# Moving a head's output gates between the two halves of its q, k, v projection

## The chip, the cores and the metric

The kernel runs on one core of a Trainium2 chip. The metric is the device time of one execution in microseconds (us), as the median of several runs; a profile is one further execution, read from its hardware trace.

## The reference, cut to what matters

One layer is computed (`DEPTH = 1`): gated differential attention over 1024 tokens, model width 1024, 16 heads with two 64-wide query/key halves and 128-wide values.

```python
h = rms_norm(x, norm_g)
q, k, v, z = jnp.split(h @ w_in, 4, axis=-1)          # 16 heads x 128 columns each
q = rms_norm(q.reshape(b, s, 16, 2, 64), q_norm_g) * 64 ** -0.5
k = rms_norm(k.reshape(b, s, 16, 2, 64), k_norm_g)
...
for blk in range(s // 128):                            # causal, ALiBi bias
    scores = einsum('bqhmd,bkhmd->bhmqk', qb, kb)
    probs = softmax(scores + bias)
    weights = probs[:, :, 0] - lam * probs[:, :, 1]
    outs.append(einsum('bhqk,bkhe->bqhe', weights, vb))
o = rms_norm(concatenate(outs), head_norm_g) * (1.0 - lam_0)
o = o.reshape(b, s, 2048) * silu(z)
return x + o @ w_out
```

The gate of a head is `silu(z)` for its 128 columns.

## The kernel before, in words

**Precision by splitting.** Each float32 operand of the projection is scaled and split in two float16 parts, high and low; a product is three matmuls (high by high, high by low, low by high). The normed input is kept transposed on chip, `hh` and `hl`, in two halves of 512 tokens (`c` = 0 and 1).

**The loop.** The main loop at the end of the function runs over the heads, odd ones first, then even ones. In turn `i` it interleaves, with `merge`, two generators: `attend` of the head before and `project` of this head. Each `yield` carries a weight, and `merge` advances whichever lags by the rates given (14.5 to 44.0). Heads 10, 12 and 14 (`LATE`) have their gates computed after the last projection, in `late_gates`; for the other 13 heads `project` computes them itself.

**project.** For each half `c`, four token blocks `t`: 24 matmuls (L404 to L406) into a PSUM tile `pg` of 384 columns (q, k, v together), then ScalarE copies q and k to `rw` (L456) and the high part of v to `vh` (L457), and VectorE makes the low part (L458). After four blocks `norm(c)` does the q, k RMSNorm: a square on ScalarE (L415), a reduction (L417), small steps (L95 to L103), a multiply (L422), the float16 split (L425, L426) and a transposing DMA into `qk` (L427) with two copies (L430). Then come the gates: `gate(..., c)` for `c` = 0 and 1, each 24 matmuls into a PSUM tile `pz` (L481 to L483) and a chain of six steps, ScalarE and VectorE in turn (L486 to L491), which reads `pz` up to its last step and leaves the gate in an SBUF tile `sz`. `pg` and `pz` share one ring of three PSUM buffers (`PSG = 3`).

**The next head's weights.** `project` also prepares the weights of the next head. `load_raw` issues eight DMAs on SyncE's queue (L136) into `raww`, of which there is one buffer. `split_w` is a generator that `prepare` advances by one step at a time: one square per block of columns on ScalarE (L160, which writes into the new `wsp` tile), a tiny matmul for the maximum (L169) into spare columns of the `pg` tile of the moment, small steps on VectorE (L172 to L185), then per block a high part on ScalarE (L206) and a low part on VectorE (q, k: L212) or GpSimd (v and gate: L209, L210). There are two `wsp` buffers. `prepare` is called after each `pg` block, and at every second step of the gates; the step with the tiny matmul can only go on where a `pg` tile is handed in, so not at the gates' calls.

**attend.** For each of eight query blocks: score matmuls (L603) into a ring of four PSUM tiles `pss`, VectorE adds the bias and takes the running minimum (L592), ScalarE the exponential (L609), VectorE and ScalarE make the weights (L612 to L619), and a DMA transposes them (L621). `values(0)` (L633 to L635) comes after block 5 and `head_norm(0)` after block 6; `values(1)` and `head_norm(1)` of a head are a tail that the next turn runs after its blocks 1 and 2. `values` ends in a copy and two squares (L639 to L644), `head_norm` in a logarithm, an exponential (L655, L656) and a multiply (L663), after which `finalize` multiplies by the gate on GpSimd (L571) and writes it to DRAM (L572).

**Who orders the engines.** The instructions of an engine are put in order before the run by a planner that simulates the engines: it takes what is ready by its own estimate, with the order of the code as priority. Code order is therefore a wish; data, buffers and the few pinned instructions are the bounds.

Of the kernel before, what the change touches and what calls it, by code (L numbers as in the profile page):

```python
# [9 lines left out]
F32 = mybir.dt.float32  # L10
# [7 lines left out]
P = 128  # L18
# [9 lines left out]
LATE = (10, 12, 14)  # L28
# [11 lines left out]
def diff_attention_kernel(  # L40
# [65 lines left out]
    heads = [h for h in range(NH) if h % 2 == 1] + [h for h in range(NH) if h % 2 == 0]  # L106
    place = {h: i for i, h in enumerate(heads)}

    with ExitStack() as main:
# [113 lines left out]
        with ExitStack() as pro:  # L223
# [65 lines left out]
            for t in range(NB):  # L289
                ht = hts[t]  # L290
                c, o = t // 4, (t % 4) * P
# [87 lines left out]
        def project(hd, wt, st):  # L379
# [52 lines left out]
            nx, prep = st["next"], []  # L432
# [12 lines left out]
                        return  # L445
                    prep.pop(0)

            for c in range(2):
                rw = tmp.tile([P, 2, 4, P], F32, name="rw", tag="rw", bufs=2)
                for t in range(4):  # L450
                    pb = ps_g.tile([P, 512], F32, name="pg", tag="pg")
                    pg = pb[:, :384]
                    for hf in range(2):
                        gemm_piece(pg, c, t * P, range(hf * 4, hf * 4 + 4))
                        if hf:
                            A.activation(rw[:, :, t], pg[:, :256].rearrange("p (s b) -> p s b", s=2), AF.Copy)  # L456
                            A.activation(vh[:, c * 4 + t], pg[:, 256:], AF.Copy, scale=vsc)  # L457
                            V.scalar_tensor_tensor(out=vl[:, c * 4 + t], in0=pg[:, 256:], scalar=vsc,  # L458
                                                   in1=vh[:, c * 4 + t], op0=ALU.mult, op1=ALU.subtract)
                            prepare(lambda: pb[:, 384:])  # L460
                        elif hd == heads[0]:
                            prepare(None)
                        yield 2.1
                norm(c, rw)
            if hd in LATE:
                while prep:
                    prepare(None)
                return
            for c in range(2):
                for k in gate(st, wt, 3, c):  # L470
                    if k % 2:
                        prepare(None)
                    yield 0.69
            while prep:
                prepare(None)

        def gate(st, wt, n, c):

            pz = ps_g.tile([P, 512], F32, name="pz", tag="pg")
            for k in range(KT):  # L480
                T.matmul(pz, wt["hi"][:, k, n], hh[c][:, k], start=k == 0, stop=False)  # L481
                T.matmul(pz, wt["hi"][:, k, n], hl[c][:, k], start=False, stop=False)  # L482
                T.matmul(pz, wt["lo"][:, k, n], hh[c][:, k], start=False, stop=k == KT - 1)  # L483
                yield k
            e = vp.tile([P, 512], F32, name="sz", tag="sz", bufs=3)
            A.activation(e, pz, AF.Exp, scale=wt["inv"][:, 1, n:n + 1])  # L486
            V.tensor_scalar(e, e, 1e18, None, ALU.min)
            A.activation(e, e, AF.Ln, bias=1.0)
            V.scalar_tensor_tensor(out=e, in0=pz, scalar=wt["inv"][:, 1, n:n + 1], in1=e, op0=ALU.mult, op1=ALU.max)
            A.activation(e, e, AF.Exp, scale=-1.0)  # L490
            V.scalar_tensor_tensor(out=e, in0=pz, scalar=wt["inv"][:, 0, n:n + 1], in1=e,  # L491
                                   op0=ALU.mult, op1=ALU.mult)
            st["z"].append(e)
# [80 lines left out]
        def attend(hd, st):  # L574
# [48 lines left out]
            def values(c, t):  # L623

                vh, vl = st["vh"], st["vl"]
                po = ps_o.tile([P, 512], F32, name="po", tag="po")
                row = 8 * (c + 1) * P
                for j in range(4 * c + 4):
                    il = max(0, j - 4 * c)
                    out = po[:, il * P:].rearrange("p (t q) -> p t q", q=P)  # L630
                    rh = view(t[:, il, j * P:], [[row, 4 - il], [1, P]])
                    rl = view(t[:, il, (4 * c + il + 1 + j) * P:], [[row + P, 4 - il], [1, P]])
                    T.matmul(out, vh[:, j], rh, start=j == 0, stop=False)  # L633
                    T.matmul(out, vl[:, j], rh, start=False, stop=False)
                    T.matmul(out, vh[:, j], rl, start=False, stop=j == 4 * c + 3)  # L635
                    if j % 2:
                        yield 6 * (4 - il) * P / 2400
                os = tmp.tile([P, 512], F32, name="os", tag="os")
                A.activation(os, po, AF.Copy, scale=st["unit"])  # L639
                sq = tmp.tile([P, 512], F32, name="sqo", tag="sqo")  # L640
                A.activation(sq, os, AF.Square)
                sqh = tmp.tile([P, 512], F32R, name="sqh", tag="sqh")
                e = V if hd == heads[-1] else G
                A.activation(sqh, os, AF.Square)  # L644
                sql = tmp.tile([P, 512], F32R, name="sql", tag="sql")
                e.tensor_tensor(sql, sq, sqh.bitcast(F32), ALU.subtract)  # L646
                pos["n"] = (os, sq, sqh, sql)
# [138 lines left out]
```

## Time and profile before

| | us |
|---|---|
| median of 3 runs (lowest, highest) | 1172.26 (1170.85, 1175.99) |
| the profiled execution, device time | 1178.97 |
| its span, first to last instruction | 1177.2 |
| TensorE (PE) busy in the span | 1114.4 (95%) |
| VectorE (DVE), ScalarE (ACT), GpSimd (POOL) busy | 910.7, 750.6, 268.8 |

The first 84 us hold the prologue and the first head's projection, which has no attention beside it. From 84 to 782 us twelve turns follow with gates and attention, some 58 us each; from 782 to 925 us the three turns of the late heads; then the late gates and the output projection. Matmuls overlap in the pipeline, so busy time is read together with the waits.

### The profile page before, as it was taken

To read this page: it belongs to the slowest core of one execution; us is meant where nothing else is said; L and a number is where in the kernel's file an instruction comes from. 1 tells how busy PE (TensorE), PEld (TensorE's weight loads), DVE (VectorE), ACT (ScalarE), POOL (GpSimd) and SP (SyncE) were. 2 spreads that over 40 slices of the span, in tenths; PEclk is the share of its full clock that TensorE was granted. 3 is DMA by queue.
4 is the path that set the end of the run, shared out by engine and by line. 5 is a ranking of instruction groups with operands and counts; after the bars stand their busy time and mean duration, and the time that the engine had idled before them with its cause. 6 is when DMAs were issued, how large, how long until landed. Compare 5 with 4: busy or idle time off the path is not lost.

```text
span 1177.2 us, 18460 instructions
## 1 busy us (share of the span) xinstructions
PE 1114.4 (95%) x6154; PEld 670.4 (57%) x6154; DVE 910.7 (77%) x2335; ACT 750.6 (64%) x1583; POOL 268.8 (23%) x210
## 2 busy tenths in 40 slices
PE   5799999999899999999999999999998987999998
PEld 3555554555455555454545555555555534788887
DVE  6877979798879798989798989797888897654111
ACT  3757678686868786868686868686768765230000
POOL 3121313131413131314131313212120302022000
PEclk7999999999999999999999999999999988999999
DMA  7343546454626364636463635263663456767342
GB/s 221 109 103 70 129 94 144 77 130 94 141 66 155 79 147 80 150 81 141 84 147 78 152 78 144 68 150 76 127 135 84 110 117 143 204 219 239 108 134 70
DMA packets 327887, 143.50 MB, mean 122 GB/s; under 512 B 225136, under 2 KB 307312, under 8 KB 327792
## 3 DMA queue, kind: packets, MB, share of 16 engines
q1 hardware_dynamic: 323040, 133.93, 47.8%
q10 hardware_dynamic: 4752, 8.39, 2.7%
q8 instruction: 48, 0.79, 0.3%
q14 instruction: 47, 0.39, 0.1%
HBM read 63.11 MB, written 16.25 MB: 67 GB/s over the span
## 4 chain that ended last, share of the span: by engine, by line
PE 49%; DVE 19%; ACT 11%; issue 7%; DMA 6%; POOL 3%; SPq 3%; ACTq 0%; DVEq 0%; POOLq 0%
PE pg L404 8%; PE pg L406 7%; PE pg L405 7%; PE pf L532 5%; PE pf L533 5%; PE pf L534 5%; DVE p L592 5%; DMA raww<-in_l_w_in_dram 3%; ACT wsp L206 3%; SPq L136 3%; PE pss L603 3%; ACT wsp L160 2%; DVE p L615 2%; ACT p L609 2%; POOL wsp L210 2%
## 5 line engine op out<-in xcount | busy, mean ns | idle before, releaser
L404 PE MATMUL pg<-wsp,h 128*128 128x384 f16 x1016 | 334.3, 329 | 9.0 <-DVE sz L491 7.3
L406 PE MATMUL pg<-wsp,h 128*128 128x384 f16 x1016 | 334.3, 329 | 2.7 <-DVE h L298 2.7
L405 PE MATMUL pg<-wsp,h 128*128 128x384 f16 x1016 | 334.1, 329 | 0.0
L609 ACT ACTIVATE p<-p,mn 128x128 f32<-128x128 f32 (+7 forms) x256 | 196.1, 767 | 39.1 <-DVE mn L592 39.0
L603 PE MATMUL pss<-qk 128*128 128x512 f16 (+3 forms) x768 | 166.5, 328 | 22.3 <-DVE mn L592 22.2
L592 DVE CUSTOM_DVE_ANT_0 p<-pss,toep,nsl 128x512 f32<-128x512 f32 (+3 forms) x256 | 160.9, 642 | 16.9 <-DMA wt<-p 8.6
L66 ACT ACTIVATE p<-p,rc 128x128 f16<-128x128 f32 (+7 forms) x128 | 98.5, 771 | 77.4 <-DVE p L615 73.6
L405 PEld LDWEIGHTS <-h 128*128 128x128 f16 x1016 | 100.0, 98 | 77.1 <-issue 17.5
L406 PEld LDWEIGHTS <-h 128*128 128x128 f16 x1016 | 100.1, 99 | 68.9 <-issue 3.0
L404 PEld LDWEIGHTS <-h 128*128 128x128 f16 x1016 | 100.0, 98 | 65.8 <-issue 4.1
L603 PEld LDWEIGHTS <-qk 128*128 128x128 f16 x768 | 70.8, 98 | 81.9 <-issue 30.3
L619 DVE SCALAR_TENSOR_TENSOR p<-p,rc,p 128x128 f16<-128x128 f32 (+7 forms) x128 | 108.5, 849 | 10.6 <-ACT p L66 9.2
L615 DVE SCALAR_TENSOR_TENSOR p<-p,rc,p 128x128 f32<-128x128 f32 (+7 forms) x128 | 108.5, 852 | 0.0
L646 POOL TENSOR_TENSOR sql<-sqo,sqh 128x512 fp32r<-128x512 f32 x30 | 41.0, 1366 | 265.0 <-ACT sqh L644 265.0
L481 PE MATMUL pz<-h,wsp 128*128 128x512 f16 x256 | 97.8, 382 | 1.5 <-DVE sz L491 1.5
L483 PE MATMUL pz<-h,wsp 128*128 128x512 f16 x256 | 97.8, 382 | 0.0
L482 PE MATMUL pz<-h,wsp 128*128 128x512 f16 x256 | 97.8, 382 | 0.0
L209 POOL TENSOR_SCALAR raww<-raww,scw 128x1024 f32<-128x1024 f32 x29 | 40.5, 1406 | 166.8 <-ACT wsp L206 142.1
L160 ACT ACTIVATE wsp<-raww 128x1024 f16<-128x1024 f32 x61 | 63.6, 1044 | 20.6 <-DMA raww<-in_l_w_in_dram 19.4
L571 POOL TENSOR_TENSOR sz<-sqo,sz 128x512 f32<-128x512 f32 x26 | 33.7, 1295 | 185.4 <-DVE sqo L663 156.2
L592 DVE CUSTOM_DVE_ANT_0 p<-pss,toep,mn 128x128 f32<-128x128 f32 (+3 forms) x128 | 75.1, 601 | 0.3 <-PE pss L603 0.3
L458 DVE SCALAR_TENSOR_TENSOR vl<-pg,vh 128x128 f16<-128x128 f32 x128 | 36.3, 284 | 45.7 <-ACT vh L457 45.5
(163 smaller groups left out, 2098.6 us busy)
## 6 DMA issues: line engine op xcount, KB each, us to landing
raww<-in_l_w_in_dram SPq DMA_DIRECT2D x96, 256.0 KB, 4.2
rawo<-in_l_w_out_dram SPq DMA_DIRECT2D x32, 256.0 KB, 4.7
qk<-qk SPq DMA_DIRECT2D x64, 128.0 KB, 2.3
raww<-in_l_w_in_dram SPq DMA_DIRECT2D x40, 192.0 KB, 3.8
g_dram<-sz SPq DMA_DIRECT2D x30, 256.0 KB, 2.3
rawg<-g_dram ACTq DMA_DIRECT2D x24, 256.0 KB, 4.1
xt<-in_x_dram SPq DMA_DIRECT2D x8, 512.0 KB, 4.5
xr<-in_x_dram SPq DMA_DIRECT2D x16, 256.0 KB, 3.4
```

What stands on the lines that cost most here:

```text
L66: A.activation(out, in_, AF.Copy, scale=scale)
L404: T.matmul(pg, a_h, w_h, start=k == 0, stop=False)
L405: T.matmul(pg, a_h, w_l, start=False, stop=False)
L406: T.matmul(pg, a_l, w_h, start=False, stop=k == KT - 1)
L481: T.matmul(pz, wt["hi"][:, k, n], hh[c][:, k], start=k == 0, stop=False)
L482: T.matmul(pz, wt["hi"][:, k, n], hl[c][:, k], start=False, stop=False)
L483: T.matmul(pz, wt["lo"][:, k, n], hh[c][:, k], start=False, stop=k == KT - 1)
L592: V.tensor_tensor_reduce(out=pm[m][:, o:o + w], in0=pss[:, :w], in1=toep[:, u:u + w], scale=nslope, scalar=3e38 if prev[m] is None else pr ...
L603: T.matmul(pss[m][:, :w].rearrange("p (t q) -> p t q", q=P), qk[:, c, 0, i % 4, m], qk[:, b, v, :w // P, m], start=v == 1, stop=v == 2)
L609: A.activation(pm[m][:, :n], pm[m][:, :n], AF.Exp, scale=-1.0, bias=prev[m], accum_out=sx[:, m:m + 1])
L615: V.scalar_tensor_tensor(out=p0, in0=p1, scalar=rc[:, 1:2], in1=p0, op0=ALU.mult, op1=ALU.add)
L619: V.scalar_tensor_tensor(out=pl[:, n:], in0=p0, scalar=rc[:, 0:1], in1=pl[:, :n], op0=ALU.mult, op1=ALU.subtract)
```

## The change

`project` runs `qkv(0)`, then both gates (not for late heads), then `qkv(1)`. `prepare` is called twice per block in `qkv(0)` of every head and once per block in `qkv(1)`. `sz` gets a fourth buffer, and the 512-wide tile `sqo` of `values` is taken from the ring of `norm`'s tile (`sqk`, two buffers).

```diff
-            for c in range(2):
+            def qkv(c):
                 rw = tmp.tile([P, 2, 4, P], F32, name="rw", tag="rw", bufs=2)
                 for t in range(4):
...
                             prepare(lambda: pb[:, 384:])
-                        elif hd == heads[0]:
+                        elif c == 0:
                             prepare(None)
                         yield 2.1
                 norm(c, rw)
-            if hd in LATE:
-                while prep:
-                    prepare(None)
-                return
-            for c in range(2):
-                for k in gate(st, wt, 3, c):
-                    if k % 2:
-                        prepare(None)
-                    yield 0.69
+            yield from qkv(0)
+            if hd not in LATE:
+                for c in range(2):
+                    for k in gate(st, wt, 3, c):
+                        if k % 2:
+                            prepare(None)
+                        yield 0.69
+            yield from qkv(1)
             while prep:
                 prepare(None)
...
-            e = vp.tile([P, 512], F32, name="sz", tag="sz", bufs=3)
+            e = vp.tile([P, 512], F32, name="sz", tag="sz", bufs=4)
...
-                sq = tmp.tile([P, 512], F32, name="sqo", tag="sqo")
+                sq = tmp.tile([P, 1024], F32, name="sqo", tag="sqk", bufs=2)[:, :512]
```

## Rows read from the trace of the kernel before

**Rows 1.** The page's busy time of each engine, share and instructions.
```profile
PE 1114.4 (95%) x6154; PEld 670.4 (57%) x6154; DVE 910.7 (77%) x2335; ACT 750.6 (64%) x1583; POOL 268.8 (23%) x210
```

**Rows 2.** Stretches: length, busy by engine (PE, PEld, DVE, ACT, POOL), PEclk, DMA, GB/s.
```profile
200.00:258.00 58.00, 56.08 (x320) 31.00 (x319) 47.22 (x125) 42.90 (x93) 15.05 (x10) 0.97 0.54 117
...
491.00:513.00 22.00, 20.22 (x121) 11.43 (x120) 19.77 (x57) 18.25 (x44) 1.27 (x1) 1.00 0.60 120
...
523.00:549.00 26.00, 26.00 (x144) 13.88 (x143) 25.05 (x66) 19.85 (x39) 12.13 (x8) 1.00 0.53 131
...
84.00:782.00 698.00, 677.35 (x3924) 377.96 (x3922) 595.83 (x1578) 528.24 (x1119) 179.21 (x119) 1.00 0.50 111
```

**Rows 3.** Waits of PE, 84 to 782: total us, times, longest us.
```profile
PE pss L603 <- DVE mn L592: 11.2, 11, 1.6
PE pg L404 <- DVE sz L491: 7.3, 8, 2.3
```

**Rows 4.** Waits of PE, 20 to 84.
```profile
PE pg L406 <- DVE h L298: 2.7, 1, 2.7
PE tp L295 <- DVE nlam L361: 2.6, 1, 2.6
```

**Rows 5.** Chain that ended last, around 441 and 499: start us, us, what.
```profile
440.80 0.32 PE pg L404
...
481.56 2.14 POOL wsp L210
...
488.40 5.42 DMA raww<-in_l_w_in_dram
...
494.56 3.23 ACT wsp L160 x6
497.79 0.53 ACT sz L490
...
499.15 0.32 PE pg L404
```

**Rows 6.** Groups by line, 84 to 782: count | busy us, mean ns | idle before.
```profile
L417 DVE TENSOR_REDUCE ssk<-sqk 128x16 f32<-128x1024 f32 x24 | 29.1, 1213 | 6.5 <-ACT sqk L415 6.5
L95 DVE TENSOR_SCALAR v_k<-ssk,ep 128x8 f32<-128x8 f32 x48 | 28.5, 637 | 0.4
L422 DVE TENSOR_TENSOR rw<-rw,r_k 128x1024 f32<-128x1024 f32 x24 | 30.1, 1255 | 1.2
L426 DVE TENSOR_TENSOR sqk<-rw,sqk 128x1024 f16<-128x1024 f32 x24 | 33.9, 1414 | 1.8 <-ACT sqk L425 1.8
L487 DVE TENSOR_SCALAR sz<-sz 128x512 f32<-128x512 f32 x24 | 10.8, 452 | 1.0 <-ACT sz L486 0.9
L489 DVE SCALAR_TENSOR_TENSOR sz<-pz,inv,sz 128x512 f32<-128x512 f32 x24 | 17.8, 743 | 0.4 <-ACT sz L488 0.4
L491 DVE SCALAR_TENSOR_TENSOR sz<-pz,inv,sz 128x512 f32<-128x512 f32 x24 | 17.9, 746 | 2.7 <-ACT sz L490 2.5
L212 DVE SCALAR_TENSOR_TENSOR wsp<-raww,scw,wsp 128x1024 f16<-128x1024 f32 x24 | 29.7, 1279 | 0.8 <-ACT wsp L206 0.8
```

**Rows 7.** Timeline, the split of one head: DVE and ACT.
```profile
526.15 0.15 DVE L172 TENSOR_SCALAR topw<-pg 128x4 f32<-128x4 f32 x1
...
531.00 4.25 ACT L206 ACTIVATE wsp<-raww,scw 128x1024 f16<-128x1024 f32 x4
```

**Rows 8.** Timeline, buffers of `sqk`, `sqo` and `sz`: ACT, POOL, SyncE's queue.
```profile
479.05 1.06 ACT L415 ACTIVATE sqk<-rw 128x1024 f32<-128x1024 f32 x1
...
498.44 1.15 SPq L430 DMA_DIRECT2D qk<-qk  x2
...
496.72 1.27 POOL L571 TENSOR_TENSOR sz<-sqo,sz 128x512 f32<-128x512 f32 x1 [10.57 <-DVE sqo L663]
...
516.57 1.06 ACT L415 ACTIVATE sqk<-rw 128x1024 f32<-128x1024 f32 x1
...
524.50 0.36 SPq L572 DMA_DIRECT2D g_dram<-sz  x1
```

## The prediction

> **What bounds the kernel now.** I read the engine shares first, then the stretches, then TensorE's waits, then the chain that ended last. TensorE is busy 95% of the span, VectorE 77% [rows 1]. In the twelve turns that hold gates and attention, 84 to 782 us, TensorE is busy 677.35 of 698 us [rows 2], so only 698 - 677.35 = 20.7 us are idle, 1.7 us per turn. The stretches of one turn show where. A turn starts at about 491, where the first half of q, k, v follows the gates of the head before. In its first 22 us TensorE is busy 20.22 and VectorE 19.77; later, from 523 to 549, TensorE has 26.00 of 26 and VectorE 25.05 [rows 2]. So the loss sits at the seam between two turns, and VectorE comes to that seam with its queue full.
>
> Two waits make up most of it: the score matmuls wait 11.2 us in 11 places for VectorE to empty a `pss` tile (L592), and the projection waits 7.3 us in 8 places for the last step of the gates (L491), because a new `pg` tile needs the PSUM buffer that a gate's `pz` still holds [rows 3]. Two stretches of 58 and 60 us, each with one of the longest waits for L491, have a mean granted clock of 0.97 and not 1.00 (one of the two rows is shown) [rows 2]; TensorE runs at 1.2 GHz there for a short while after the wait. At 0.03 of 58 us that is 1.7 us each, 3.4 us.
>
> The chain shows why L491 is late [rows 5]. GpSimd ends the split of the next head's weights at 481.56 + 2.14 = 483.7; only then is the one `raww` buffer free and SyncE can issue eight loads; the last is issued at 488.40 and lands 5.42 us later, at 493.8; the squares of the new weights run from 494.56 on ScalarE, in front of the gate chain's last exponential (L490, 497.79), and TensorE starts its `pg` matmuls again at 499.15. The same restart one turn before is at 440.80, so a turn takes 58.35 us. TensorE's loss is thus not lack of speed but two late arrivals at one place: the gates' evacuation, behind the weights' loads and squares, and VectorE's backlog.
>
> **The change, part by part.** No arithmetic is added or removed; the counts of all groups should stay. What counts is order and buffers.
>
> *Gates moved ahead of qkv(1).* By the weights in the code a projection is 16.8 (half 0) + 11.0 (gates) + 16.8 (half 1) = 44.6. The gates end at 27.8, where 44.6 was the end; what follows them is `qkv(1)`, not the next turn. Of the three PSUM buffers two are then `pz`; block 0 of `qkv(1)` takes the third and block 1 needs the first `pz`. The chain that empties it costs VectorE 0.45 + 0.74 + 0.75 = 1.94 us [rows 6] and has, from the end of gate 0, the 5.5 of gate 1, the 4.2 of block 0 and the attention between. In the old place the distance was the same; what differs is the company: no weight loads land there and no squares run. So the 7.3 us should go. Bounds 0 (it all comes back at the middle) and -7.3; I take -7.3. With it go the two clock stretches, -3.4 (bounds 0, -3.4). What is late next at the seam is L592.
>
> *norm(1) moved to the end.* The gates stood behind it and covered its chain; now the next turn covers it. Its VectorE part is 1.21 + 2 x 0.64 + 1.26 + 1.41 = 5.2 us [rows 6], and it comes beside the largest softmax block. Its result, half 1 of `qk`, is read by the scores from block 4 on, some 29 us into the turn (attention weights up to block 4, 7.4, plus the projection's 21.6). From square to the two copies the chain took 479.05 to 498.44, 19.4 us [rows 8], and the copies some 2 us more: nobody should wait for it. It moves 5.2 us of VectorE to the seam, less the part that already ran there.
>
> *The split moved ahead.* With two calls of `prepare` per block in half 0, the fifth call makes the maxima ready and the sixth, at block 2, carries the tiny matmul; before, that was block 0 of half 1, and the trace has its reader L172 at 526.15, 35 us after the seam [rows 7]. It comes some 18 us earlier. The rest follows: ScalarE's four high parts, 4.25 us in one burst at 531.00 [rows 7], VectorE's two low parts, 2 x 1.28 = 2.6 us [rows 6], GpSimd's share. VectorE so loses 2.6 us in its full stretch (25.05 of 26) and gains it nearer the front; with both gate chains there (3.9 us, before half at the seam) and norm(1) gone from it, that stretch is lighter by about 2.6 + 5.2 - 3.9 = 3.9 us at most. A wait of the 11.2 us group is 1.6 us at the longest [rows 3], so a backlog lighter by a part of 3.9 us could remove many. Bounds 0 and -11.2; I take half, -5.6, since norm(1) now stands in the seam's own queue. The eight loads follow GpSimd, so they are issued in the middle of the turn, queued on SyncE ahead of some transposes of that stretch, about 5 us (483.7 to 488.40); they land some 15 us before the squares, which wait for the old `wsp` buffer till the turn ends. The squares stay at the seam as a 4 us burst, but the gate chain is no longer behind them: behind them now are the copies of the last `pg` tiles and the exponentials.
>
> *New waits.* The trace does not show what the planner makes of the new middle, nor what four squares do in front of block 0's exponentials. Bounds: 0, and +11.2, a second group as large as the one of L592; I take +4, a third of it, since TensorE had no idle time at all in the middle (26.00 of 26 [rows 2]) and the ring has the distance counted above.
>
> *First head.* Its projection has no attention beside it, and TensorE waits 2.7 and 2.6 us for the normed input and the prologue's last steps [rows 4]. Gate 0 needs only half 0 of the input and can now fill such holes. Against that, the next head's maxima wait for `qkv(1)` as before, so nothing is earlier for the second head. Bounds 0 and -5.3; I take -4.
>
> *Late heads, buffers.* Late heads gain only an earlier split, nothing (bounds 0, -2). `sz`: two gates of this head, two of the head before, and one older, whose write to DRAM is issued at 524.50, 33 us into the turn [rows 8]; gate 1 ends at 27.8 + some 9.4 of attention = 37, so four buffers do, with 4 us between them for the write to land. `sqk`: a rival, below.
>
> Sum: -7.3 - 3.4 - 5.6 - 4 + 4 = -16.3. The sum is made against the profiled execution, 1178.97 (span 1177.2 and 1.8 around it), which gives 1162.7. That execution is 6.7 above the median of the runs, so the median after should be 1172.3 - 16.3 = 1156.
>
> **The rivals.**
>
> *The loss moves (the same).* norm(1) at the seam costs VectorE 5.2 us where the gate chains cost 3.9. If that, and not the loads, keeps L592 late, the group of 11.2 us doubles while 7.3 and the first head's 4 are saved: 1172.3 + 11.2 - 11.3 = 1172. For it: VectorE has 19.77 of 22 us there now. Against it: the lighter stretch before.
>
> A rule points the same way. TensorE is the engine with the highest share, and its work stays as it is [rows 1]. The Trainium skill, Perfetto Trace Analysis, section Identifying the Most-Contended Engine, says to speed up the most-contended engine first, and that matmul busy time is a poor measure of how close TensorE is to its limit. By its first half this change does nothing: 1172. The idle 20.7 us at one place of the turn [rows 2] speak against that reading, and no more than these and the clock's share can be won.
>
> *The ring of sqk blocks ScalarE (slower).* Two buffers now serve norm(0), values(0), norm(1) and values(1). norm(1) starts at the seam, and with the 19.4 us from square to copies [rows 8] it gives its buffer back 20 us into the next turn; values(0) gives the other back when GpSimd is done, 496.72 + 1.27 = 498, 7 us into it; values(1) and then norm(0) ask for both by 516.57, 25 us into it [rows 8]. That is 5 us to spare. It decides from the point where norm(1)'s chain takes over 24 us. ScalarE then stands at L415 or L641 with the copies of `pg` queued behind it, and after three `pg` tiles TensorE stands too. At 27 us that is 3 us in each of 12 turns, 36 us, against the 20.3 us saved without new waits: 1172.3 + 36 - 20.3 = 1188. For it: norm(1)'s VectorE steps join a full queue. Against it: the 19.4 us were already taken in a full queue.
>
> *It does not do what it says (the same).* The planner may lay the instructions much as before, as order in code is only a priority. Then 1172. Against it: the tiny matmul needs a `pg` tile of a given block, and that is data.
>
> **How the numbers follow.** The forecast has 0.62, with a range of its own of 1146 to 1166. The moved loss has 0.18, no effect 0.05, the blocked ring 0.15. About 0.5% is what a measurement of this kernel can tell from no change, so faster is below 1166.4 and slower above 1178.1: 0.62, 0.23, 0.15. All gains at their far bounds and no new wait give 1172.3 - 7.3 - 3.4 - 11.2 - 5.3 = 1145 (1143 with the late heads); the bounds of new waits with nothing saved would give 1183. The range of 1146 to 1177 leaves out the ring and a little at the low end, under 2 in 10.
>
> **What would show it.** In the changed profile: in the turns with gates PE's wait for L491 gone or under 2 us in all; ScalarE's squares waiting for no load; L172 near 17 us into a turn and the loads in its middle; the clock at 1.00 in all stretches; PE's wait for L592 near 6 us. Wrong would be: L592's group over 15 us, ScalarE waiting at L415, L641 or L486 for a DMA, or a new wait of PE in `qkv(1)`.

## The result and the profile after

The changed kernel takes 1181.39 us (median of 5 runs, 1180.37 to 1183.9) against 1172.26 (5 runs, 1169.13 to 1175.99) of the kernel before: a ratio of 1.0077, 95% interval 1.0049 to 1.0105. It is slower by 9 us, where 16 us less were forecast, and lies above the range. The profiled execution of after took 1181.39 (span 1179.6), its median; that of before lay 6.7 above its own median, so the two traces differ by only 2.4 us of span. In the changed kernel the line numbers behind L480 are smaller by one: L490 is the gates' last step (L491 before), L591 the minimum (L592), L602 the scores (L603), L632 the values (L633).

The page's busy time, the line that answers to [rows 1]:

```profile
PE 1114.7 (95%) x6154; PEld 668.0 (57%) x6154; DVE 929.5 (79%) x2335; ACT 747.4 (63%) x1583; POOL 280.6 (24%) x210
```

The counts are the same, as they should be. But VectorE is busy 18.8 us longer and GpSimd 11.8 us longer with the same instructions: some of them take longer.

A turn runs from the first `pg` matmul of one head to that of the next. Below, first before, then after: the first head's turn (from 20 us, in the prologue), the second turn, the third, and the ten turns up to the late heads. The columns are those of [rows 2]: length, busy time of PE, PEld, DVE, ACT, POOL, then PEclk, DMA share, GB/s.

```profile
20.00:83.90 63.90, 54.37 (x303) 31.44 (x304) 50.48 (x127) 37.92 (x86) 18.93 (x14) 0.88 0.36 101
83.90:137.50 53.60, 51.84 (x307) 29.24 (x305) 44.85 (x125) 39.31 (x85) 10.28 (x7) 1.00 0.44 89
137.50:194.60 57.10, 56.44 (x332) 31.55 (x330) 48.37 (x129) 41.65 (x93) 17.64 (x12) 1.00 0.50 114
194.60:782.00 587.40, 569.17 (x3295) 317.24 (x3293) 502.71 (x1326) 447.27 (x943) 151.29 (x102) 0.99 0.51 113
```

```profile
20.00:88.90 68.90, 54.88 (x313) 32.83 (x314) 51.31 (x142) 41.30 (x97) 14.09 (x12) 0.88 0.27 76
88.90:148.70 59.80, 54.04 (x295) 28.93 (x294) 49.64 (x124) 40.03 (x84) 18.02 (x10) 0.94 0.60 134
148.70:208.60 59.90, 56.72 (x329) 31.31 (x327) 46.89 (x114) 40.22 (x83) 14.28 (x9) 1.00 0.43 94
208.60:784.90 576.30, 566.75 (x3294) 315.35 (x3292) 510.59 (x1322) 439.27 (x938) 160.45 (x103) 1.00 0.51 113
```

The front (these first three turns) loses 5.0, 6.2 and 2.8 us, 14.0 in all. The ten steady turns win 11.1: TensorE's idle time there falls from 587.40 - 569.17 = 18.2 us to 9.6, and the other 2.4 us are busy time: before has two stretches of 3.4 us at 1.2 GHz in these turns (at 202.1 and 325.0), after has none. What lies behind 785 us differs by only 0.5 us between these two traces. So the change does its work in the steady part and loses more in three turns at the front.

How sure is the steady gain? A second profiled execution of the kernel before (below, 1173.92 us) has 586.2 us for those ten turns, the gain then being 9.9; there the part behind them was 391.8 us, against 395.2 in the first trace and 394.7 after. The front's loss against it is 14.5. These add up to the difference of its span, 1172.1 against 1179.6. The last part differs by 3.4 us between two executions of the same kernel; that is about half of the 6.7 us by which the first trace of before lies above its median. Over all the traces of the experiments below, the ten steady turns take 573.6 to 578.1 us in the seven kernels that have the gates in the middle, and 583.1 to 587.4 in the four traces of the old order with the old buffers. The gain is clear; its size is 5 to 14 us, by the pair that is taken.

**The steady part.** TensorE's waits from 209 to 785 us after, which answer to [rows 3] (total us, times, longest; two more of 0.3 and 0.2 us are left out), and behind them the minimum's wait in the ten steady turns of before:

```profile
PE po L632 <- DMA wt<-p: 7.3, 10, 2.0
PE pmn L652 <- POOL sql L645: 0.9, 2, 0.5
PE pg L404 <- DVE sz L490: 0.5, 1, 0.5
...
PE pss L603 <- DVE mn L592: 9.7, 10, 1.6
```

Both waits of [rows 3] are as good as gone: in the same stretch of before they are the 9.7 us for L592 and all of the 7.3 for L491. A new one has come, 7.3 us in 10 places, in which the values wait for the transposed weights. SyncE's queue shows why (start, duration, operation; the stretch 466 to 482), and the chain's row for the same transposes stands behind it:

```profile
468.23 2.63 SPq L136 DMA_DIRECT2D raww<-in_l_w_in_dram  x4
471.26 1.40 SPq L620 DMA_TRANSPOSE wt<-p  x1
472.71 2.61 SPq L136 DMA_DIRECT2D raww<-in_l_w_in_dram  x4
475.42 6.63 SPq L620 DMA_TRANSPOSE wt<-p  x2
...
471.26 10.27 DMA wt<-p x2
```

The eight loads of the next weights now stand among the transposes, at the middle of the turn. The three transposes of this stretch took 4.5, 6.1 and 3.0 us from issue to landing; over the ten turns of before the fastest took 2.3, the median 3.0 and the slowest 6.8. TensorE stood 2.04 us, until 481.58, for the one that took 6.1. Some 6.5 of the 7.3 us are like this: eight waits end with a transpose that was issued while four or five of the loads were in flight, 4.4 to 6.1 us before it landed. Before had slow ones too (13 were issued beside loads, with a median of 4.3 us against 2.9 for the others), but no wait of TensorE ended with one.

**The first turn.** TensorE's two longest waits, 20 to 89 us after; they answer to [rows 4]:

```profile
PE tp L295 <- DVE htok L271: 10.5, 2, 9.4
PE pg L398 <- ACT wsp L206: 5.6, 2, 3.8
```

The wait of 9.4 us is new (the 5.6 us for L398 are in both). On TensorE's timeline it stands here, with what comes before and after it:

```profile
50.74 0.38 PE L482 MATMUL pz<-h,wsp 128*128 128x512 f16 x1
52.75 1.06 PE L295 MATMUL tp<-ident,htok 128*128 128x128 f32 x8 [1.63 <-DVE nlam L361]
63.17 1.94 PE L295 MATMUL tp<-ident,htok 128*128 128x128 f32 x8 [9.36 <-DVE htok L271]
...
65.11 0.63 PE L480 MATMUL pz<-h,wsp 128*128 128x512 f16 x1
65.54 0.53 PE L404 MATMUL pg<-wsp,h 128*128 128x384 f16 x1
```

Gate 0 ends at 51; then nothing but the prologue's transposes runs until 65, when the last block of the normed input is transposed and gate 1 and half 1 start together. Before, `pg` matmuls of half 1 fill part of this place, one block from 46.7 to 50.8 and one from 57.1 to 63.7; their first rows in the trace of before:

```profile
46.73 0.33 PE L406 MATMUL pg<-wsp,h 128*128 128x384 f16 x1
...
57.11 0.50 PE L406 MATMUL pg<-wsp,h 128*128 128x384 f16 x1 [2.69 <-DVE h L298]
```

A `pg` block needs only its own block of the input. Gate 1 needs all four blocks of half 1, and its `pz` tile stands before half 1's `pg` tiles in the ring of three PSUM buffers. Counted in code order, block 0 of half 1 takes the ring's buffer that the last block of half 0 gave back at 47.07 (the end of its L458), so no occupied buffer held it; still its first matmul stands right behind gate 1's first, at 65.54. Gate 1's place in the order is what holds it (run 3). Whether it does so because the ring's tiles are given out in code order or by the planner's priority, no run tells. Block 1 takes gate 0's buffer, and that came free late too: in after the last step of gate 0's chain, L490, ends at 65.00, among the prologue's steps on VectorE and ScalarE.

From 57.1, within the hole, to 67.3 TensorE was granted half its clock, 1.2 GHz; before has 6.8 us of that in this turn, from 55.3. In the second turn the same comes from 132.2 to 139.0:

```profile
57.10:67.30 10.20, 4.13 (x17) 2.98 (x18) 7.57 (x15) 6.15 (x13) 0.00 (x0) 0.50 0.35 79
132.20:139.00 6.80, 4.81 (x17) 2.36 (x18) 6.80 (x17) 5.45 (x11) 1.27 (x1) 0.50 1.05 274
```

**The second turn.** Up to 118 TensorE is busy 28.3 of 29.1 us. The two stretches behind that:

```profile
118.00:132.00 14.00, 11.24 (x56) 5.19 (x53) 14.00 (x25) 9.46 (x18) 9.79 (x5) 1.00 0.30 67
132.00:148.70 16.70, 14.51 (x77) 8.23 (x78) 14.35 (x36) 10.48 (x24) 1.27 (x1) 0.80 1.02 215
```

From 118 to 132, just behind the gates, VectorE is full (14.00 of 14) and GpSimd busy for 9.79; TensorE has 11.24 of 14. TensorE's waits in this turn are 5.6 us in all, the longest 2.3 in three places for the minimum and 1.9 in one for the copies of `qk`, both between 129 and 134. In before no stretch of this turn behind 100 us leaves TensorE idle. Of the 6.2 us that the turn loses, 4.0 are idle time (5.8 against 1.8) and 2.2 busy time, with the 6.8 us at half the clock.

### The profile page after: what moved, and what is told of

Its sections match the earlier page's. It is cut to its first block, busy times and chain, and to the rows that moved or that the text cites. A ratio compares the mean times of both kernels' runs of the same rounds, so it can differ in the third digit from the quotient of the medians.

```text
span 1179.6 us, 18332 instructions
## 1 busy us (share of the span) xinstructions
PE 1114.7 (95%) x6154; PEld 668.0 (57%) x6154; DVE 929.5 (79%) x2335; ACT 747.4 (63%) x1583; POOL 280.6 (24%) x210
## 4 chain that ended last, share of the span: by engine, by line
PE 48%; DVE 21%; DMA 11%; ACT 8%; issue 8%; SPq 1%; POOL 1%; ACTq 0%; DVEq 0%; POOLq 0%
PE pg L405 7%; PE pg L404 7%; PE pg L406 7%; DVE p L591 6%; DMA wt<-p 6%; PE pf L533 5%; PE pf L532 5%; PE pf L531 5%; PE pss L602 3%; ACT wsp L160 2%; DVE wsp L212 2%; DVE p L614 2%; ACT p L608 2%; PE po L632 2%; PE po L634 2%
## 5 line engine op out<-in xcount | busy, mean ns | idle before, releaser
L602 PE MATMUL pss<-qk 128*128 128x512 f16 (+3 forms) x768 | 169.2, 329 | 9.5 <-DVE mn L591 7.5
L591 DVE CUSTOM_DVE_ANT_0 p<-pss,toep,nsl 128x512 f32<-128x512 f32 (+3 forms) x256 | 159.9, 641 | 16.5 <-DMA wt<-p 10.6
L404 PEld LDWEIGHTS <-h 128*128 128x128 f16 x1016 | 100.0, 98 | 66.3 <-issue 1.7
L614 DVE SCALAR_TENSOR_TENSOR p<-p,rc,p 128x128 f32<-128x128 f32 (+7 forms) x128 | 116.9, 913 | 0.0
L602 PEld LDWEIGHTS <-qk 128*128 128x128 f16 x768 | 71.5, 98 | 74.5 <-issue 14.0
L480 PE MATMUL pz<-h,wsp 128*128 128x512 f16 x256 | 98.4, 384 | 0.8 <-DVE sz L490 0.8
L570 POOL TENSOR_TENSOR sz<-sqo,sz 128x512 f32<-128x512 f32 x26 | 41.7, 1603 | 192.0 <-DVE sqo L662 98.5
L591 DVE CUSTOM_DVE_ANT_0 p<-pss,toep,mn 128x128 f32<-128x128 f32 (+3 forms) x128 | 75.1, 602 | 0.0
L206 ACT ACTIVATE wsp<-raww,scw 128x1024 f16<-128x1024 f32 (+1 forms) x65 | 67.9, 1110 | 9.4 <-DVE scw L180 9.3
L632 PE MATMUL po<-wt,vh 128*128 128x512 f16 x192 | 63.3, 330 | 11.0 <-DMA wt<-p 7.7
```

What stands on the lines that cost most here:

```text
L404: T.matmul(pg, a_h, w_h, start=k == 0, stop=False)
L591: V.tensor_tensor_reduce(out=pm[m][:, o:o + w], in0=pss[:, :w], in1=toep[:, u:u + w], scale=nslope, scalar=3e38 if prev[m] is None else pr ...
L602: T.matmul(pss[m][:, :w].rearrange("p (t q) -> p t q", q=P), qk[:, c, 0, i % 4, m], qk[:, b, v, :w // P, m], start=v == 1, stop=v == 2)
L614: V.scalar_tensor_tensor(out=p0, in0=p1, scalar=rc[:, 1:2], in1=p0, op0=ALU.mult, op1=ALU.add)
```

## The experiments

All kernels of one group ran beside the kernel before on the same chip. "Seam" is the first `pg` matmul of a turn, and the lengths of turns are worked out from these starts. The expectations call the theories by letters. F: the whole loss is in the first head's turn. M: the second turn loses because the first head's attention has no tail of an older head with it; its weights in the code sum to 9.7 (the expectations say 9.4) against 14.0 of a full turn, so at the rate 14.5 to 44.0 it is done at 9.7 x 44 / 14.5 = 29 of the projection's 44.6, with its largest blocks beside the gates (16.8 to 27.8), and half 1 of the projection then runs nearly alone. R: the shared `sqk` ring costs time, the prediction's second rival. D: the split at double pace draws out VectorE's operations beside GpSimd, so that the front loses wherever the attention lies. S, G and P are told where they stand.

**1. Only the first head in the old order.**

```diff
-                        elif c == 0:
+                        elif c == 0 or hd == heads[0]:
...
+            parts = ([qkv(0), qkv(1)] if hd in LATE else [qkv(0), qkv(1), gates(0), gates(1)] if hd == heads[0] else
+                     [qkv(0), gates(0), gates(1), qkv(1)])
...
```

> The changed kernel, but the first head alone keeps the order of the kernel before (both halves of q, k, v, then both gates) and its calls of prepare; all other heads have the gates in the middle. Theory F (the loss is made in the first head: gate 1 stands ahead of half 1 in the ring of three PSUM buffers, needs the whole normed input, and so holds back half 1's blocks until the prologue ends): the first two seams come back from 88.9 and 148.7 us to about 84 and 138, no wait of 9.4 us for the last normed block, and the time falls by 10 to 14 us below the changed kernel, to 1168 to 1172, a ratio to the kernel before of 0.996 to 1.000. Rival S (every turn pays for norm(1) at the seam and for the loads in its middle; the front is only cut differently): less than 4 us are won back, 1177 to 1182, ratio 1.004 to 1.008.

Measured: 1181.59 us, 1.0084 (1.0063 to 1.0104). The first, second and third turn and the ten steady ones:

```profile
20.00:83.00 63.00, 53.22 (x302) 30.95 (x303) 50.54 (x127) 38.28 (x87) 19.22 (x14) 0.89 0.37 102
83.00:149.30 66.30, 55.48 (x307) 30.21 (x305) 51.70 (x128) 40.92 (x87) 12.62 (x7) 0.92 0.47 109
149.30:209.80 60.50, 57.01 (x334) 31.61 (x332) 49.28 (x127) 42.16 (x90) 14.36 (x9) 1.00 0.42 88
209.80:783.40 573.60, 565.98 (x3293) 315.39 (x3290) 509.95 (x1319) 438.92 (x938) 160.98 (x103) 1.00 0.50 114
```

The first turn is as before, and nothing is won: the second turn takes 66.3 us, 6.5 more than after. Theory F falls. Rival S has the time right but not the cause: its steady turns take 573.6 us, the least of all. In the second turn TensorE waits 6.2 us at one place for the gates' last step and 4.4 for the minimum. VectorE and GpSimd at that time:

```profile
118.38 3.24 DVE L212 SCALAR_TENSOR_TENSOR wsp<-raww,scw,wsp 128x1024 f16<-128x1024 f32 x1
...
122.14 2.55 DVE L212 SCALAR_TENSOR_TENSOR wsp<-raww,scw,wsp 128x1024 f16<-128x1024 f32 x1
...
118.41 5.19 POOL L210 TENSOR_TENSOR wsp<-raww,wsp 128x1024 f16<-128x1024 f32 x2
```

L212 took 1.28 us on average before [rows 6]. So the second turn loses at its middle with the first head in the old order too.

**2. Only the first head in the new order; the buffers as in the change.**

```diff
-                        elif c == 0:
+                        elif hd == heads[0] and c == 0:
...
+            parts = ([qkv(0), qkv(1)] if hd in LATE else [qkv(0), gates(0), gates(1), qkv(1)] if hd == heads[0] else
+                     [qkv(0), qkv(1), gates(0), gates(1)])
...
```

> The reverse: only the first head has the gates in the middle, with its calls of prepare; all other heads are as in the kernel before; buffers of sz and sqk as in the changed kernel. Theory F: slower than the kernel before by the whole front loss, 10 to 14 us, 1182 to 1187, ratio 1.009 to 1.012, with the wait of about 9 us for the last normed block. Rival S: within 4 us of the kernel before.

Measured: 1201.25 us, 1.025 (1.0231 to 1.027), a miss for both theories. The first turn is that of after (seam at 88.9), the second takes 51.5 and the third 57.0, but all the steady ones 59 to 63. TensorE's waits from 197 to 800 us:

```profile
PE pss L604 <- DVE mn L593: 16.3, 14, 2.2
PE pg L404 <- DVE sz L492: 15.8, 10, 2.4
```

The first head costs the 5 us that it costs in after. The ten steady turns, 197.4 to 809.0, lose 24 us against before's 587.4. These turns differ from before in the new buffers alone, unless the first head's shift moved their plan. Run 5 takes that by itself.

**3. First head: gate 0 early, gate 1 last.**

```diff
...
+            parts = ([qkv(0), qkv(1)] if hd in LATE else [qkv(0), gates(0), qkv(1), gates(1)] if hd == heads[0] else
+                     [qkv(0), gates(0), gates(1), qkv(1)])
...
```

> The changed kernel, but the first head runs half 0, gate 0, half 1, gate 1; the other heads have both gates in the middle. Gate 0 still fills the holes of the prologue, and no pz tile that waits for the whole input stands ahead of half 1. If it is gate 1's place in the ring that holds half 1 back (theory F), the wait of 9.4 us goes, the first seam comes to 82 to 85 us and the time is as with the first head in the old order or 1 to 3 us better, 1166 to 1172. If instead gate 0's chain on VectorE and ScalarE delays the prologue (rival G), the first seam stays at 87 to 90 us and the time at 1178 to 1182.

Measured: 1171.9 us, 1.0001 (0.9987 to 1.0015). First and second turn:

```profile
20.00:79.30 59.30, 52.91 (x303) 31.57 (x304) 48.80 (x124) 37.19 (x85) 18.76 (x14) 0.92 0.31 87
79.30:141.30 62.00, 55.53 (x311) 30.64 (x308) 52.97 (x149) 44.45 (x99) 15.65 (x8) 0.92 0.60 136
```

The hole of 9.4 us is gone; the wait for L271 is 1.9 us in three places. The turn ends at 79.3, 9.6 us before that of after and 4.6 before that of the old order. The second turn again takes more, 62.0, with one wait of 5.6 us for GpSimd's squares' low part (`pmn` L654 for `sql` L647). Against after the median falls by 9.5 us. So gate 1's place makes the hole, rival G falls (gate 0 is still early), and the second turn is a loss of its own. Runs 8 and 10 have the same first head and their first seams at 80.5 and 82.0; the traces with the old first head have it at 83.0 to 83.9.

**4. The kernel before once more**, unchanged, for a second trace.

> The kernel before, profiled once more. The prediction took the two turns of 60.6 and 62.1 us (the others 57 to 59), with their low clock, as the kernel's own. If they are (rival), two or more turns of over 60 us show again and the sum of the turns from the third to the end of the thirteenth, 194.6 to 781.9 us, stays near 587 us. If they were that one execution's (its time is 6.7 us over the median), no turn is over 60 us and the same stretch is 578 to 583 us.

Measured: 1173.92 us (one run; span 1172.1). The turn of 62.1 us in the first trace is long again, 62.7; the one of 60.6 takes 59.1, and there is one stretch at the lower clock (6.8 us, at 320.3) and not two. The ten steady turns take 586.2 us, 1.2 less than in the first trace, so their length is the kernel's own, as the prediction took it. A long turn with a stretch at the lower clock is not the old order's alone: runs 8 and 10 have one of 61.0 us each.

**5. The old order with the new buffers alone.**

```diff
-            e = vp.tile([P, 512], F32, name="sz", tag="sz", bufs=3)
+            e = vp.tile([P, 512], F32, name="sz", tag="sz", bufs=4)
...
-                sq = tmp.tile([P, 512], F32, name="sqo", tag="sqo")
+                sq = tmp.tile([P, 1024], F32, name="sqo", tag="sqk", bufs=2)[:, :512]
```

> The kernel before with nothing changed but the buffers: sz has four, and the sqo tile of values comes from norm's ring of two. The run with only the first head changed had turns of 60 to 63 us from the third on, where the kernel before has 57 to 59, and differs there in these buffers alone. Theory R (the shared ring of two costs time, as it ties values to norm): 3 us a turn in some ten turns, 1195 to 1203, ratio 1.02 to 1.026. Rival P (the first head's shift moved the later turns' plan, the buffers are free): 1170 to 1176.

Measured: 1195.91 us, 1.0218 (1.0187 to 1.0248; the kernel before on this chip 1170.07). The nine turns from the fourth seam on, and the same nine of before behind them:

```profile
253.40:806.10 552.70, 524.29 (x2965) 289.68 (x2963) 456.35 (x1188) 400.54 (x845) 144.60 (x92) 0.97 0.47 107
```

```profile
255.20:781.90 526.70, 511.03 (x2965) 285.06 (x2963) 452.79 (x1192) 402.98 (x850) 136.24 (x92) 1.00 0.50 112
```

They lose 26.0 us, 2.9 a turn: 28.4 - 15.7 = 12.7 of it idle time, 13.3 busy time at the lower clock (0.97). The waits of [rows 3] grow to some 3 us in each turn (15.3 us for L592 and 13.1 for L491). So the new buffers cost 2.9 us a turn in the old order, with the first head as in before, and rival P falls. That it is the shared ring and not the fourth `sz` buffer is argued; the two edits were not run apart. The way is not the one that the prediction named: ScalarE waits for no buffer at L415, and at L641 0.4 us, for L639.

**6. The change with a `sqo` buffer of its own.** The space is taken from the output projection, which has five raw tiles and not six.

```diff
-                sq = tmp.tile([P, 1024], F32, name="sqo", tag="sqk", bufs=2)[:, :512]
+                sq = tmp.tile([P, 512], F32, name="sqo", tag="sqo")
...
```

> The changed kernel with its gates in the middle, but values' sqo tile has a buffer of its own again (to make room, the ring of the output projection's raw tiles, used from about 925 us on, has five buffers and not six; so the seams of the turns before that are compared). Theory R: the shared ring is also what slows the second and third turn (59.8 and 59.9 us, before 53.6 and 57.2) and leaves some of the later ones over 57: seams at 781.9 (before) and 784.9 (changed) become 770 to 776 and the time 1168 to 1174. Rival D (VectorE, held up by GpSimd in the denser middle, is what slows the second and third turn): they stay at 59 to 60 us and the seam at 782 to 786.

Measured: 1178.09 us, 1.0067 (1.0044 to 1.009). The seams are those of after (89.0, 148.1, 208.3, and 784.6 at the end), and TensorE waits as there:

```profile
PE po L632 <- DMA wt<-p: 8.9, 9, 1.8
```

Up to 784.6 us the shared ring costs nothing in the new order; R falls as a cause of the 9 us.

**7. The old order with the split at double pace.**

```diff
-                        elif hd == heads[0]:
+                        elif hd == heads[0] or c == 0:
```

> The kernel before with nothing changed but the calls of prepare: twice per block in half 0 for every head, so that the split, its loads and squares come earlier, with gates and buffers as before. If the steady turns' gain of the changed kernel (57.5 us and not 58.4) comes from the weights' earlier loads, the waits for L491 at the seam go and the turns fall to 57 to 57.7, 1163 to 1168. If it comes from the gates' place, the turns stay at 58 to 59 and the time at 1170 to 1175.

Measured: 1174.34 us, 1.0032 (1.0013 to 1.0051). The second, third and the ten steady turns:

```profile
83.80:139.20 55.40, 52.69 (x306) 29.06 (x304) 48.26 (x124) 38.56 (x84) 14.23 (x8) 1.00 0.46 103
139.20:199.60 60.40, 56.92 (x333) 31.59 (x332) 48.55 (x132) 42.78 (x94) 15.28 (x9) 1.00 0.49 113
199.60:786.30 586.70, 569.18 (x3294) 317.55 (x3292) 505.97 (x1324) 445.39 (x941) 145.58 (x102) 0.99 0.49 112
```

The earlier split alone wins nothing in the steady part (586.7 against 587.4 and 586.2), so what is won there needs the gates' new place. Whether it needs the earlier split as well is open: the new order with the old pace was not run. The earlier split costs 1.8 us in the second and 3.3 us in the third turn. The third turn takes 59.0 to 60.5 us in the traces of all eight kernels with the double pace in every head, and 57.0 to 58.0 in the five other traces: that is the 2.8 us of after's third turn.

**8. Runs 3 and 6 together.**

> Both at once: first head in the order half 0, gate 0, half 1, gate 1, the others with the gates in the middle, and an own buffer for sqo (with five raw tiles in the output projection). The order of the first head alone won 9.5 us over the changed kernel. If the ring costs time as well (theory R), another 5 to 10 us, 1162 to 1168, ratio 0.991 to 0.996; if not (rival D), 1169 to 1174.

A miss: 1177.73 us, 1.0064 (1.0039 to 1.0089). The front is that of run 3 (seams 80.5, 141.4, 201.4) and the last full turn ends at 778.4, 3.5 us earlier than before. The first turn of the late heads takes 43.6 us as in before. The next turn and the stretch from there to the output projection's first matmul take 53.2 and 103.3 us, 156.5 together; run 6 has 157.2, and all the kernels with six raw tiles between 144 and 152. So the output projection's smaller buffering eats what the front gives; that it is the raw tiles is argued from the two runs that share the edit. That an own `sqo` would do no harm with all six raw tiles was not run, as the space isn't there.

**9. The change with a slower attention in the second turn.** The rate is 9.7 to 44.0 there, so that the first head's attention lasts as long as the projection.

```diff
-                merge(att, project(heads[i], wt, st), *(RATE if i < NH - 1 else RATE_LAST))
+                merge(att, project(heads[i], wt, st), *((9.7, 44.0) if i == 1 else RATE if i < NH - 1 else RATE_LAST))
```

> The changed kernel, but in the second turn, where the first head's attention has no tail of an earlier head beside it, merge's rate for attention is 9.7 and not 14.5 (9.7 is 14.5 by the ratio of the weights, 9.4 of 14.0). Theory M: at the common rate this short attention is over at 28 of the projection's 44.6, so its largest blocks fall beside the gates once these stand at 16.8 to 27.8, VectorE falls behind, and qkv(1) then runs alone. Spread over the turn, the second turn falls from 59.8 to 53 to 56 us, TensorE's waits in it from 5.6 to under 2, and the time by 4 to 7 us to 1174 to 1178. Rival D (GpSimd's split in VectorE's way, whatever the attention's place): the second turn stays at 59 to 60 and the time at 1180 to 1183.

Measured: 1175.77 us, 1.0035 (1.0016 to 1.0053; before 1171.15). The second turn from 118 us on, to be read beside that of after:

```profile
118.00:132.00 14.00, 10.61 (x56) 5.54 (x54) 14.00 (x21) 9.38 (x18) 8.60 (x5) 0.91 0.33 71
132.00:145.40 13.40, 13.40 (x81) 7.79 (x80) 11.42 (x28) 8.61 (x17) 2.11 (x1) 0.97 1.13 251
```

The turn is 56.1 us, 3.7 less than after, where M asked for 53 to 56 and D for 59 to 60; TensorE's waits in it are 4.1 us, where M had under 2. The hole from 118 to 132 has stayed (3.4 us, TensorE now waiting for the squares of `values`), but the end of the turn is full, 13.40 of 13.4, where after has 14.51 of 16.7. Less attention at the middle helps, as M says; it does not mend VectorE's full stretch there.

**10. Runs 3 and 9 together: gate 1 last in the first head, slower attention in the second turn.** The diff is the two of those runs.

> The first head in the order half 0, gate 0, half 1, gate 1, and the slower rate of attention in the second turn; all other heads with the gates in the middle. Theory M with the gate-1 finding: both front losses are gone, second turn 53 to 57 us (62.0 with the first of the two alone), 1163 to 1168, ratio 0.992 to 0.997 to the kernel before. Rival D: 1170 to 1174.

Measured: 1165.01 us, 0.9947 (0.9927 to 0.9968; before 1171.15). It is 6 us faster than the kernel before and faster than the change. First, second, third and steady turns:

```profile
20.00:82.00 62.00, 54.53 (x302) 32.10 (x303) 48.29 (x127) 37.61 (x87) 19.23 (x14) 0.89 0.31 87
82.00:140.50 58.50, 54.58 (x306) 30.12 (x305) 50.09 (x127) 40.29 (x86) 11.86 (x7) 0.94 0.57 129
140.50:199.50 59.00, 56.76 (x334) 31.66 (x332) 48.05 (x129) 42.47 (x91) 15.29 (x10) 1.00 0.48 102
199.50:777.60 578.10, 568.25 (x3294) 317.09 (x3292) 500.75 (x1319) 436.74 (x938) 152.36 (x102) 1.00 0.50 113
```

The front takes 179.5 us against 174.6 before and 188.6 after, the ten steady turns 578.1 against 587.4. So the time came as M forecast, but the front's loss is not all gone: the second turn is 58.5 us and not the 53 to 57 of the expectation, with one wait of 3.9 us for the gates' last step. Its last full turn so ends 4.4 us earlier than before's; both profiled executions lie alike above their medians, by 6.1 and 6.7 us.

**11. The control: the old order with the slower attention.**

```diff
-                merge(att, project(heads[i], wt, st), *(RATE if i < NH - 1 else RATE_LAST))
+                merge(att, project(heads[i], wt, st), *((9.7, 44.0) if i == 1 else RATE if i < NH - 1 else RATE_LAST))
```

> The kernel before with the slower rate of attention in the second turn alone, as a control. In the old order the short attention ends at 28 of 44.6, in half 1, and the gates run behind it with little else on VectorE. Theory M says that nothing is to be won here: second turn 53 to 56 us, 1170 to 1176, ratio 0.998 to 1.003. If the slower rate helps by itself (rival), it gains 4 us or more here too.

Measured: 1174.01 us, 1.0023 (1.0008 to 1.0039). The second turn takes 55.4 us, 1.8 more than before. So the rate does not help by itself; it helps where the gates stand in the middle. Its ten steady turns take 583.1 us, so with run 4 the gain of the new order in these turns lies between 6.8 and 11.1 us, according to which trace of the old order it is held against.

## Why the prediction was wrong

**The steady turns: the sum right, its terms not, so in part by luck.** Their part of the sum was -7.3 - 3.4 - 5.6 + 4 = -12.3; measured -11.1, and -6.8 to -9.9 against other traces of the old order. The gates' wait (-7.3) went down to 0.5. The clock's -3.4 came as some -2.4: before's two stretches of 3.4 us at 1.2 GHz went (TensorE busy for 6.4 of the 6.8 us, so 3.2 at most was to be had), and the busy time fell by 2.4. The wait for L592 was sized at half its group and went altogether, 9.7 us in this stretch. "New waits" stood at +4; it is 7.3 us for the transposes and 1.4 in small ones, and the cause isn't the one that was named (squares in front of block 0's exponentials): it is the eight loads in SyncE's queue, which the prediction placed ahead of transposes and costed at nothing. Two terms were each some 4 us off, and the two errors cancel.

**Places: right.** L172 comes at 167.09 and 226.53, 18 us into their turns (17 forecast), the loads in the middle and the squares wait for no load. One sign of the wrong list is there: ScalarE waits at the gates' first step (L485, L486 before) for the write of `sz`, from 209 to 785 us:

```profile
ACT sz L485 <- DMA g_dram<-sz: 7.3, 5, 1.8
```

The 4 us that the prediction left between the fourth buffer's reuse and the write were thus used up in half of the ten turns; before has this wait as well, 2.9 us in five. No wait in TensorE's list is put down to it, and at L415 and L640 ScalarE waits for no ring.

**First head: the step that failed by its sign.** It stood at -4, "gate 0 ... can now fill such holes", with bounds 0 and -5.3. Gate 0 did fill one. The step left out that gate 1 moves too, that it needs the whole of half 1's input, and that half 1's `pg` blocks come behind it in the order. The result is a wait of 9.4 us and +5.0 for the turn. The bound should have had a positive end, as the trace of before showed `pg` blocks of half 1 at work in just that place. Run 3, which moves gate 0 alone, has -4.6 at the first seam, near the forecast -4; with runs 8 and 10, at 80.5 and 82.0, it is 1 to 5 us against the traces of the old order.

**Second turn: the step that was not there.** The sum took the twelve turns as alike. The first has an attention without tail and, in before, the only short turn (53.6 us), so it had cover to lose: with the gates in the middle, its largest blocks, the split and both gate chains meet in 118 to 132, where VectorE is full. It costs 6.2 us. Run 9 gave back 3.7 of them by the rate alone, run 11 showed that the rate alone is worth nothing, and run 7 has 1.8 us of the loss with the earlier split alone.

**Third turn: "late heads gain only an earlier split, nothing" and its like for the early ones.** The split at double pace was costed at nothing or a gain. Run 7 shows no gain in the steady part and 5.1 us of loss in the second and third turn. After's third turn has 3.2 us of TensorE's time idle against 0.7 before, in small waits of at most 1.1 us for three different operations. Why they come with the split's pace, the traces did not tell; that stays open.

**The rivals.** "The loss moves" did not come: L592 is quiet, so norm(1) at the seam is no burden. The blocked ring was priced at 3 us a turn, and run 5 has 2.9, but that is luck: it comes in the old order, where the prediction did not look for it, and without ScalarE standing at L415 or L641, the way that was priced. Why the buffers cost time there and not in the new order stays open too. The slower outcome came by a mechanism that was no rival: work at the program's front, where the steady order does not hold yet. "It does not do what it says" was wrong.

The sum of what was measured: 5.0 + 6.2 + 2.8 - 11.1 - 0.5 = +2.4 between the two traces, and 14.5 - 9.9 + 2.9 = +7.5 against the second trace of before, whose time is nearer its median; the medians say +9.1.

## What to carry to other kernels

Cost a change of a loop's order for the first turns apart from the steady ones: there the data come late, the work beside it is shorter, and a step moved ahead may need more than the step it passes. Ask of each moved step which input it needs in full: here a block that was ready stood 18 us behind a gate that was not, though no occupied buffer held it. And follow each moved load to the queue it joins, for small transfers behind it wait too.

## What the runs showed of the hardware

Some of VectorE's operations last longer while GpSimd works. In before, the two L95 at 518.91, where GpSimd's last operation ends at 518.97, took 0.36 us together; those at 482.71, beside GpSimd, took 2.24 and ended with GpSimd's instructions. The reduction L417 ran beside GpSimd just before them and took its usual time, 1.21 us; at 48.10, with GpSimd idle, it took 1.20.

```profile
480.98 1.21 DVE L417 TENSOR_REDUCE ssk<-sqk 128x16 f32<-128x1024 f32 x1
...
482.71 2.24 DVE L95 TENSOR_SCALAR v_k<-ssk,ep 128x8 f32<-128x8 f32 x2
...
518.91 0.36 DVE L95 TENSOR_SCALAR v_k<-ssk,ep 128x8 f32<-128x8 f32 x2
...
478.76 4.93 POOL L210 TENSOR_TENSOR wsp<-raww,wsp 128x1024 f16<-128x1024 f32 x2
483.65 1.26 POOL L419 TENSOR_TENSOR rw<-rw,gain 128x512 f32<-128x512 f32 x1
```

The Trainium skill, SBUF — State Buffer, section SBUF: two separate sides, says that VectorE and GpSimd share a pair of ports as an exclusive lock, which one instruction holds for its whole length, and that a VectorE instruction needs it in a two-port mode or with two inputs in SBUF. The trace agrees on the lock: the L95 end at 483.71 and 484.94, within 0.1 us of GpSimd's 483.69 and 484.91.

Summed over VectorE's operations, the time above the 20th percentile of the same form (counted where it is over 0.05 us) is 54 us before and 77 after, and all of it falls on operations that ran beside one of GpSimd's. In the second turn it goes from 1.2 to 5.4 us, and each steady turn has 1.2 more. The growth of 23 us covers the 18.8 us by which VectorE's busy time rose without an instruction more. It does not belong to the new order as such: run 10 has 57 us. That TensorE pays for it only where VectorE is full, at the front, is argued from the waits above.
